# Scores and pair products of an SSD layer: when they are put into TensorE's stream of weight products, and in which order the weight blocks come

## The chip, the core and the metric

The kernel runs on one core of a Trainium2 chip. The metric is the device time of one execution in microseconds (us). Five engines work side by side, each through its own queue in program order: TensorE (PE, matrix products; its weight loads are listed as PEld), VectorE (DVE), ScalarE (ACT), GpSimd (POOL, here it mostly issues DMAs) and SyncE (SP, which issues the weight loads). An instruction waits at the head of its queue for the others' results, and everything behind it waits with it.

## The reference, cut to what matters

256 positions, width 2048: one Mamba-2 (SSD) layer of 64 heads in 8 groups, then keys and values and one attention layer, then a norm.

```python
def mamba2_layer(h, w_in, conv_w, conv_b, dt_bias, A_log, D_skip, gnorm_g, w_out):
    proj = h @ w_in                                  # 2048 x 10304
    z, xbc, dt = ...                                 # 4096, 6144 (x 4096, B 1024, C 1024), 64
    xbc = silu(causal_depthwise_conv(xbc, conv_w, conv_b))
    xs, bm, cm = ...                                 # 8 groups: x of 8 heads x 64, B and C of 128
    dt = softplus(dt + dt_bias); a = dt * -exp(A_log)
    y = ssd_chunked_scan(xs * dt, a, bm, cm)         # one chunk of 256
    y = y + D_skip * xs
    y = grouped_rmsnorm(y * silu(z), gnorm_g, 8)
    return y @ w_out                                 # 4096 x 2048

# in the scan, of the one chunk:
    a_cum = cumsum(ac, axis=1)
    decay = exp(where(causal, a_cum[l] - a_cum[s], -inf))      # per head
    cb = einsum("blgn,bsgn->blsg", cc, bc)                     # per group: the "scores"
    y_diag = einsum("blsgr,bsgrp->blgrp", cb * decay, xc)      # per head: the "pairs" multiply this

# reference(): x + mamba2_layer(rmsnorm(x)), then K and V of it, the attention layer, the last norm
```

## The kernel before, in words

**Weight products.** All weights are read from HBM once. A unit of work is one load of two 128-row slices of 512 columns (`load`, on SP, 512 KB). ACT rounds it to a reduced format (`hi`), DVE takes the rest (`lo`), both in `split`; then PE makes 12 products of 128x512 (`products`: two slices, two halves of the positions, and hi, lo and hi again against the two parts of the operand). In the trace these products are `ps<-hi,hT`, `ps<-lo,hT`, and with `yn`, `kvop`, `bop` or `oop` in place of `hT` for the later layers. Four raw buffers, five of `hi` and `lo`; splits are written three units ahead.

**Blocks.** `ORDER` (line 36) lists the blocks of the SSD layer. B, C, x, z and a number are 512 columns of the input projection, 8 units or 96 products each; d0 is the one of dt. o0 to o3 and o10 to o13 are quarters of the first half of the output projection, 4 units or 48 products each: o0 to o3 need the normed groups 0 and 1 (yn0, yn1), o10 to o13 need yn2 and yn3. p0 to p3 are the second half, 96 products each, which need yn4 to yn7. `late` (line 283) changes the start of p: first 6 units of p0, 6 of p1, then the last two units of each; so the first product that reads yn7 is product 144 after the start of p0.

**Side work.** Everything else of the layer is written as generators that `Side` advances between the products: `conv_gen` (convolution and SiLU of B, C and x, then x transposed and times dt, `xd`), `cb_gen` (the four score matrices of four groups, `cb`; PE reads C and B out of buffers named xs, so a visit to it reads `s<-xs`), `pair_gen` (two heads at a time: a DMA on POOL spreads the running sums over a buffer `em`, ACT makes the decays of it, DVE multiplies by the scores, PE makes the heads' output `s<-em,xd`, DVE adds D·x and multiplies by the gate z), `z_gen` (the gate), `norm_gen` (squares, a transposed sum `s<-ident,squares`, a chain of small DVE operations on `nt`, its result transposed back `s<-ident,nt`, the normed y into `yn`). There are two `em` buffers and four PSUM banks `s`. I call it a visit when PE leaves the products for such a piece and comes back.

**What sets the order.** While the program is written, a model keeps a time for PE, ACT and DVE (`Clock`, `Paced`), and `Side.some` (line 156) takes the next piece of a generator only where its last work ended, by the model, at least `MARGIN` (750 ns) before PE's time. A generator gives that time by what it last did itself, or by a number that it yields; where it yields a condition, the model knows only that it is fulfilled, not when the other generator's result is there. Before the products of a unit whose operand has not been written yet, all side work is forced through (line 1154): it is then put ahead of the unit, ready or not.

```python
            if entry[2] <= PE.ns - MARGIN:
                most -= self.advance(entry)
...
        if need not in st:
            force(lambda: need in st)
```

Of the kernel before, what the change touches and what calls it, by code (L numbers as in the profile page):

```python
# [15 lines left out]
P = 128  # L16
L = 256
# [15 lines left out]
MARGIN = 750.0  # L33


ORDER = "B0 d0 C0 x0 z0 x1 z1 x2 z2 x3 z3 B1 C1 x4 o0 z4 o1 x5 o2 z5 o3 x6 o10 z6 o11 x7 o12 z7 o13 p0 p1 p2 p3".split()
LOAD = 4700.0
WRITE = 5000.0
READ = 7000.0
# [132 lines left out]
def trunk_kernel(ctx: ExitStack, tc: tile.TileContext, x, a_norm_g, a_w_in, a_conv_w, a_conv_b,  # L172
# [3 lines left out]
    clock = Clock()  # L176
# [22 lines left out]
    PE = Paced(clock, nc.tensor, pe_cost, 0.0)  # L199
# [18 lines left out]
    B = {}  # L218
# [5 lines left out]
    def of(tag):  # L224
        return next(s for s in (banks, S[0], spare) if tag in s.shape)

    def can(*tags):
        return lambda: all(of(t).free(t) > 0 for t in tags)

    def take(tag):  # L230
        return of(tag).take(tag)
# [3 lines left out]
    def give(*tiles):  # L235

        for t in tiles:
            key = t.tensor.name, t.offset
            freed.append((next(s for s in (banks, S[0], spare) if key in s.held), key, clock.last))
# [17 lines left out]
    def copied(t, begin=0.0, issue=700.0):  # L257

        copies[0] = max(PE.ns, copies[0], begin) + issue
        clock.put(clock.writes, clock.part(t), copies[0] + READ, POOL)  # L260
        return copies[0] + READ
# [136 lines left out]
    def by_channel(U):  # L398

        return U.rearrange("p (b j l) -> p j b l", b=8, j=4)  # L400

    def in_32s(a):
        return a.rearrange("p j (b l) -> p j b l", l=32)
# [12 lines left out]
    em = take("em")  # L416
# [66 lines left out]
    for h in range(4):  # L483
        ACT.activation(early[:, 0, :512], xl[0][:, h * 512:(h + 1) * 512], AF.Square, accum_out=ss[:, 0, h:h + 1])
        v = xl[1][:, h * 512:(h + 1) * 512]
# [43 lines left out]
    hT = big.tile([P, 16, 2 * L], F32R, name="hT", tag="op")  # L529
    yn = {}  # L530
    st = {}

    def normed(i):

        c = slice(i * 512, (i + 1) * 512)
        DVE.tensor_scalar(xl[0][:, c], xl[0][:, c], r0[:, 0:1], None, op0=OP.mult)
        if i == 0:
            DVE.tensor_scalar(xl[1][:, c], xl[1][:, c], r0[:, 1:2], None, op0=OP.mult)
        else:
            ACT.activation(xl[1][:, c], xl[1][:, c], AF.Copy, scale=r0[:, 1:2])  # L540
# [63 lines left out]
    def conv_gen(U, there, c, key, group=None):  # L604

        yield there
        yield can("u", "xs")
        u, v = take("u"), take("xs")
        ACT.activation(in_32s(u), by_channel(U), AF.Copy)
        give(U)  # L610
        yield
        for j in range(4):
            k = 3 * 48 + c + j
            ACT.activation(v[:, j, :], u[:, j, :], AF.Identity, bias=cbias[:, c + j:c + j + 1], scale=cw[:, k:k + 1])
        for i in (1, 2, 3):
            yield
            for j in range(4):
                k = (3 - i) * 48 + c + j
                DVE.scalar_tensor_tensor(v[:, j, i:], u[:, j, :L - i], cw[:, k:k + 1], v[:, j, i:],
                                         op0=OP.mult, op1=OP.add)  # L620
        yield
        ACT.activation(u, v, AF.Tanh)
        yield
        DVE.scalar_tensor_tensor(v, u, 1.0, v, op0=OP.add, op1=OP.mult)
        give(u)
        st[key] = v
        if group is None:
            return
        yield lambda: "dal" in st and can("xd")()
        xd = take("xd")  # L630
        for i in (0, 2):
            yield can("s")
            p = take("s").rearrange("p (t c) -> p t c", t=2)
            for e in range(2):
                for t in range(2):
                    PE.transpose(p[:, t, e * P:(e + 1) * P], v[:, i + e, t * P:(t + 1) * P], ident)
            yield
            h = 2 * (c + i)
            DVE.tensor_mul(xd[:, :, i * P:(i + 2) * P].rearrange("p t (h c) -> p t h c", h=4),
                           p.rearrange("p t (h c) -> p t h c", h=4),  # L640
                           st["dal"][:, :, h:h + 4, None].to_broadcast([P, 2, 4, 64]))
            give(p)
        st["xd", group] = xd

    def conv_evac(c, key, group=None):
        def evac(ps, t):
            U, there = turn(ps, t)
            if t:
                side.add(conv_gen(U, there, c, key, group))
        return evac  # L650

    def cb_gen(q):
        B, C = st.pop(("B", q)), st.pop(("C", q))
        for j in range(4):
            yield can("s", "cb")
            p, cb = take("s")[:, :384], take("cb")
            PE.matmul(p[:, 0:256], lhsT=B[:, j, 0:P], rhs=C[:, j, :], start=True, stop=True)
            PE.matmul(p[:, 256:384], lhsT=B[:, j, P:L], rhs=C[:, j, P:L], start=True, stop=True)
            yield
            DVE.tensor_mul(cb, p, tri)  # L660
            give(p)
            st["cb", 4 * q + j] = cb
        give(B, C)

    def c_evac(q):
        base = conv_evac(40 + 4 * q, ("C", q))

        def evac(ps, t):
            base(ps, t)
            if t:  # L670
                side.add(cb_gen(q), lambda: ("B", q) in st and ("C", q) in st)
        return evac

    def pair_gen(g, j):

        c = 4 * g + j
        E = take("em")
        AC = st["AC"]
        R = bass.AP(tensor=AC.tensor, offset=AC.offset + 2 * c * L, ap=[[0, P], [L, 2], [1, L]])
        POOL.dma_start(E[:, :, :L], R)  # L680
        yield copied(E)
        yield lambda: "dal" in st
        dal = st["dal"]
        for h in range(2):
            a = 64 + 2 * c + h
            ACT.activation(E[:, h, 256:384], E[:, h, P:L], AF.Relu, bias=dal[:, 1, a:a + 1], scale=-1.0)
            ACT.activation(E[:, h, 0:256], E[:, h, 0:256], AF.Relu, bias=dal[:, 0, a:a + 1], scale=-1.0)
        ACT.activation(E, E, AF.Exp, scale=-1.0)
        yield lambda: ("cb", g) in st
        DVE.tensor_mul(E, E, st["cb", g][:, None, :].to_broadcast([P, 2, 384]))  # L690
        yield lambda: ("xd", g) in st and can("s")() and (("y", g) in st or can("yt")())
        xd, xs = st["xd", g], st["xs", g]
        q = take("s")[:, :L]
        for h in range(2):
            PE.matmul(q[h * 64:(h + 1) * 64, :], lhsT=xd[:, 0, j * P + h * 64:j * P + (h + 1) * 64],
                      rhs=E[:, h, 0:256], start=True, stop=False)
        for h in range(2):
            PE.matmul(q[h * 64:(h + 1) * 64, P:L], lhsT=xd[:, 1, j * P + h * 64:j * P + (h + 1) * 64],
                      rhs=E[:, h, 256:384], start=False, stop=True)
        give(E)  # L700
        if ("y", g) not in st:
            st["y", g], st["n", g] = take("yt"), 0
        yield
        y = st["y", g][:, j, :]
        DVE.scalar_tensor_tensor(y, xs[:, j, :], Dv[:, c:c + 1], q, op0=OP.mult, op1=OP.add)
        give(q)
        st["x", g] = st.get(("x", g), 0) + 1
        if st["x", g] == 4:
            give(xs, xd, st["cb", g])
        yield lambda: ("z", g) in st  # L710
        z = st["z", g]
        y = y.rearrange("p (b l) -> p b l", l=32)
        DVE.scalar_tensor_tensor(y, y, 0.5, by_channel(z)[:, j], op0=OP.mult, op1=OP.mult)
        st["n", g] += 1
        if st["n", g] == 4 and g not in (1, 3):
            give(z)
# [59 lines left out]
    def x_evac(g):  # L776
        base = conv_evac(4 * g, ("xs", g), g)

        def evac(ps, t):
            base(ps, t)  # L780
            if not t:
                return
            for j in range(4):
                side.add(pair_gen(g, j), lambda: "AC" in st and can("em")())
            side.add(norm_gen(g), lambda: st.get(("n", g)) == 4)
        return evac
# [23 lines left out]
    def x1_load():  # L810
        B["x1"] = [big.tile([P, D], F32, name=f"x1{t}", tag=f"y{7 - t}") for t in range(2)]
        for t in range(2):
            POOL.dma_start(B["x1"][t], xv[:, t])
        copies[0] = max(PE.ns, copies[0]) + 1200.0
        yield copies[0] + READ
        st["x1"] = True
# [73 lines left out]
    side.add(x1_load(), lambda: st.get(("n", 3)) == 4)  # L890
    for name in ORDER:
        kind, i = name[0], int(name[1:])
# [6 lines left out]
        else:  # L899
            n = i % 10  # L900
# [164 lines left out]
    for kind, n in ("z0", "q0", "z1", "q1", "z2", "q2", "q3", "z3"):  # L1065
        n = int(n)
# [136 lines left out]
```

## Time and profile before

| what | value |
|---|---|
| median of 3 runs | 1174.68 us (1172.6 to 1178.49) |
| the profiled execution's own time | 1174.74 us |
| its span, first to last instruction | 1173.0 us |
| PE busy | 1147.5 us, 98% of the span |
| PEld, DVE, ACT, POOL busy | 930.5, 835.0, 628.3, 107.2 us |
| PE in the chain that ended last | 87% |

The profile counts an engine as busy from an instruction's start to its modelled end, and PE's products overlap, so PE's 98% doesn't say that only 2% could be saved. What does is the distance between the starts of neighbouring products: where it is longer than in an undisturbed stretch, PE did something else or nothing. A bracket at the end of a row of the timeline is the time for which the engine stood idle before it and what ended that.

### The profile page before, as it was taken

The numbers are of one execution on the slowest core, as the hardware profiler recorded it, in microseconds if no ns is written. First come the engines' busy times: TensorE is split into PE (matmuls) and PEld (weight loads), VectorE is DVE, ScalarE is ACT, GpSimd is POOL, SyncE is SP. The second block draws the span as 40 slices with busy tenths as digits, with TensorE's granted clock in tenths as the row PEclk, the third lists the DMA queues.
The fourth block names the chain that finished last, engine by engine and source line by source line (L and its number), as shares of the span: only waits on it lengthen the run. The fifth ranks groups of instructions, "written<-read, shape, count | busy, mean of one in ns | idle before, by whom it ended". The sixth has DMA issues, their size and how long they took to land.

```text
span 1173.0 us, 14915 instructions
## 1 busy us (share of the span) xinstructions
PE 1147.5 (98%) x5285; PEld 930.5 (79%) x5285; DVE 835.0 (71%) x1275; ACT 628.3 (54%) x866; POOL 107.2 (9%) x185
## 2 busy tenths in 40 slices
PE   7999999999999999999998999999999999999996
PEld 4787877777778787887876888888888888888885
DVE  5786968788888678687776468777444677678564
ACT  5556565677656555655653555443443453544553
POOL 2011021111210011100010000000000000100000
PEclk9999999999999999999998999999999999999998
DMA  6787878778796777776774366778757767677552
GB/s 214 222 233 219 251 220 242 239 233 246 234 300 201 211 237 228 234 224 204 223 247 146 114 217 206 233 217 241 223 169 239 225 200 223 206 213 239 171 182 90
DMA packets 127658, 252.61 MB, mean 215 GB/s; under 512 B 12320, under 2 KB 12400, under 8 KB 127200
## 3 DMA queue, kind: packets, MB, share of 16 engines
q1 hardware_dynamic: 118064, 222.86, 60.5%
q0 software_dynamic: 9520, 28.81, 9.7%
q8 instruction: 41, 0.67, 0.2%
q14 instruction: 33, 0.27, 0.1%
HBM read 232.69 MB, written 18.94 MB: 215 GB/s over the span
## 4 chain that ended last, share of the span: by engine, by line
PE 87%; DMA 4%; DVE 4%; ACT 3%; issue 2%; SPq 0%; POOL 0%; ACTq 0%; DVEq 0%
PE ps L128 81%; PE s L128 6%; DMA raw<-in_a_w_in_dram 2%; DVE xs L128 1%; ACT hi L128 1%; DVE lo L128 1%; DMA raw<-in_a_w_out_dram 1%; ACT xs L128 1%; DMA U<-turned 1%; DMA turned<-T 0%; SPq L412 0%; DVE nt L128 0%; ACT em L128 0%; DVE T L128 0%; DVE yt L128 0%
## 5 line engine op out<-in xcount | busy, mean ns | idle before, releaser
L128 DVE TENSOR_TENSOR lo<-raw,hi 128x1024 fp32r<-128x1024 f32 x384 | 462.2, 1217 | 218.6 <-ACT hi L128 217.6
L128 ACT ACTIVATE hi<-raw 128x1024 fp32r<-128x1024 f32 x384 | 398.2, 1054 | 298.8 <-PE ps L128 181.2
L128 PE MATMUL ps<-hi,hT 128*128 128x512 f32 x1280 | 412.5, 395 | 0.1
L128 PEld LDWEIGHTS ps<-hi,hT 128*128 128x128 f32 x1280 | 240.3, 188 | 52.9 <-issue 3.6
L128 PE MATMUL ps<-lo,hT 128*128 128x512 f32 x640 | 249.6, 390 | 0.0
L128 PE MATMUL ps<-hi,yn 128*128 128x512 f32 x512 | 167.5, 398 | 3.0 <-ACT yn L128 2.9
L128 PE MATMUL ps<-hi,bop 128*128 128x512 f32 x512 | 164.0, 395 | 0.0
L128 PE MATMUL ps<-hi,kvop 128*128 128x512 f32 x512 | 159.0, 390 | 0.0
L394 POOL DMA_DIRECT2D U<-turned x128 | 74.2, 586 | 908.4 <-DMA turned<-T 482.4
L128 PEld LDWEIGHTS ps<-lo,hT 128*128 128x128 f32 x640 | 120.3, 188 | 23.0
L128 PEld LDWEIGHTS ps<-hi,yn 128*128 128x128 f32 x512 | 97.1, 190 | 24.6 <-ACT yn L128 3.2
L128 PEld LDWEIGHTS ps<-hi,kvop 128*128 128x128 f32 x512 | 96.1, 188 | 19.9
L128 PEld LDWEIGHTS ps<-hi,bop 128*128 128x128 f32 x512 | 96.1, 188 | 19.7
L128 PE MATMUL ps<-lo,yn 128*128 128x512 f32 x256 | 100.8, 394 | 0.0
L128 PE MATMUL ps<-lo,bop 128*128 128x512 f32 x256 | 99.7, 389 | 0.0
L128 PE MATMUL ps<-lo,kvop 128*128 128x512 f32 x256 | 99.6, 389 | 0.0
L128 PE MATMUL ps<-hi,oop 128*128 128x512 f32 x256 | 82.4, 395 | 0.0
L128 DVE SCALAR_TENSOR_TENSOR xs<-u,cw,xs 128x255 f32<-128x255 f32 (+2 forms) x144 | 59.9, 475 | 0.1
L128 PEld LDWEIGHTS ps<-lo,yn 128*128 128x128 f32 x256 | 48.7, 190 | 9.3
L128 ACT ACTIVATE em<-em,dal 128x128 f32<-128x128 f32 (+1 forms) x128 | 54.4, 448 | 2.9 <-DMA em<-AC 0.8
L128 PEld LDWEIGHTS ps<-hi,oop 128*128 128x128 f32 x256 | 48.1, 188 | 9.8
L128 PEld LDWEIGHTS ps<-lo,bop 128*128 128x128 f32 x256 | 48.1, 188 | 9.6
(168 smaller groups left out, 903.4 us busy)
## 6 DMA issues: line engine op xcount, KB each, us to landing
raw<-in_a_w_in_dram SPq DMA_DIRECT2D x160, 512.0 KB, 5.4
raw<-in_a_w_out_dram SPq DMA_DIRECT2D x64, 512.0 KB, 4.8
raw<-in_w_kv_dram SPq DMA_DIRECT2D x64, 512.0 KB, 4.7
raw<-in_b_w_in_dram SPq DMA_DIRECT2D x64, 512.0 KB, 4.6
turned<-T SPq DMA_DIRECT2D x64, 256.0 KB, 4.7
U<-turned POOLq DMA_DIRECT2D x128, 128.0 KB, 5.5
raw<-in_b_w_out_dram SPq DMA_DIRECT2D x32, 512.0 KB, 4.5
em<-AC POOLq DMA_DIRECT2D x32, 256.0 KB, 6.7
```

Of the source, the lines that this page charges most:

```text
L128: return call(out, *args, **kw)
L394: POOL.dma_start(U[32 * q:32 * q + 32].rearrange("p (b c) -> p b c", b=8), src)
```

## The change

Three edits. `ORDER`: from x4 on, each z block comes before the o block that it stood behind, so that o0 to o12 move one place back; o12 and o13 now both follow z7. `cb_gen`: a wait in the model until both operands are ready by its clock (`when`), in place of the bare condition that they have been written. `pair_gen`: of two neighbouring pairs, the even one stops after the multiplication by the scores; the odd one waits, in the model, for `xd` and the even one's result, then for two free banks, and makes the products of both; each goes on by itself from its own bank.

```diff
-ORDER = "... z3 B1 C1 x4 o0 z4 o1 x5 o2 z5 o3 x6 o10 z6 o11 x7 o12 z7 o13 p0 p1 p2 p3".split()
+ORDER = "... z3 B1 C1 x4 z4 o0 x5 o1 z5 o2 x6 o3 z6 o10 x7 o11 z7 o12 o13 p0 p1 p2 p3".split()
...
-        st[key] = v
+        st[key], when[key] = v, clock.last
...
-        st["xd", group] = xd
+        st["xd", group], when["xd", group] = xd, clock.last
...
         B, C = st.pop(("B", q)), st.pop(("C", q))
+        yield max(when["B", q], when["C", q])
...
         DVE.tensor_mul(E, E, st["cb", g][:, None, :].to_broadcast([P, 2, 384]))
-        yield lambda: ("xd", g) in st and can("s")() and (("y", g) in st or can("yt")())
-        xd, xs = st["xd", g], st["xs", g]
-        q = take("s")[:, :L]
...
+        st["em", g, j], when["em", g, j] = E, clock.last
+        if j % 2:
+            yield lambda: ("xd", g) in st and ("em", g, j - 1) in st
+            yield max(when["xd", g], when["em", g, j - 1])
+            yield lambda: of("s").free("s") > 1 and (("y", g) in st or can("yt")())
+            for i in (j - 1, j):
+                xd, E, q = st["xd", g], st.pop(("em", g, i)), take("s")[:, :L]
...
+                give(E)
+                st["q", g, i], when["q", g, i] = q, clock.last
...
+        else:
+            yield lambda: ("q", g, j) in st
+            yield when["q", g, j]
+        xd, xs, q = st["xd", g], st["xs", g], st.pop(("q", g, j))
```

**On PE, the first scores.** Second half of block z0. Before, the first score product (`s_953<-xs_802,xs_557`: C and B of the first four groups) stands right behind the last product of the unit `hi_871`:

```order
L128 MATMUL ps_860<-lo_872,hT_130 128x512
L128 MATMUL ps_860<-hi_871,hT_130 128x512
L128 MATMUL s_953<-xs_802,xs_557 128x256
L128 MATMUL s_953<-xs_802,xs_557 128x128
L128 MATMUL ps_849<-hi_893,hT_130 128x512
```

After, six products of the next unit (`hi_893`) stand ahead of it:

```order
L128 MATMUL ps_860<-lo_872,hT_130 128x512
L128 MATMUL ps_860<-hi_871,hT_130 128x512
L128 MATMUL ps_849<-hi_893,hT_130 128x512
L128 MATMUL ps_849<-lo_894,hT_130 128x512
L128 MATMUL ps_849<-hi_893,hT_130 128x512 x2
L128 MATMUL ps_849<-lo_894,hT_130 128x512
L128 MATMUL ps_849<-hi_893,hT_130 128x512
L128 MATMUL s_965<-xs_802,xs_557 128x256
L128 MATMUL s_965<-xs_802,xs_557 128x128
```

The score visit moved back by six products. The other stretch with scores (groups 4 to 7) starts 12 products into z4 before, 78 products into z4 after; counted in products from the layer's start that is 18 later.

**On PE, a group's pairs.** Block x2. Before, one pair to a visit; behind these rows 16 more products come before the next pair (`s_1521<-em_1310,xd_1195`):

```order
L128 MATMUL ps_1445<-hi_1385,hT_130 128x512
L128 MATMUL s_1480<-em_1303,xd_1195 64x256 x2
L128 MATMUL s_1480<-em_1303,xd_1195 64x128 x2
L128 MATMUL ps_1438<-hi_1403,hT_130 128x512
L128 MATMUL ps_1438<-lo_1404,hT_130 128x512
```

After, the same two pairs in one visit:

```order
L128 MATMUL ps_1437<-hi_1431,hT_130 128x512
L128 MATMUL s_1519<-em_1321,xd_1240 64x256 x2
L128 MATMUL s_1519<-em_1321,xd_1240 64x128 x2
L128 MATMUL s_1524<-em_1328,xd_1240 64x256 x2
L128 MATMUL s_1524<-em_1328,xd_1240 64x128 x2
L128 MATMUL ps_1454<-hi_1431,hT_130 128x512
```

The 32 pairs take 27 visits before (22 of one pair, 5 of two) and 16 visits of two pairs after.

**On ACT, the last group's norm.** Blocks p0 and p1. ACT writes one `hi` for each unit of 12 products. Before, from the `hi` of the unit that starts 144 products after the start of p0 (`hi_5392`, the first unit that reads yn7) on:

```order
L128 ACTIVATE hi_5392<-raw_5298 128x1024
L128 ACTIVATE squares_5412<-yt_5203 128x1024
L128 ACTIVATE hi_5414<-raw_5326 128x1024
L128 ACTIVATE hi_5434<-raw_5346 128x1024
L128 ACTIVATE hi_5455<-raw_5366 128x1024
L128 ACTIVATE yn7_5483<-yt_5203 128x4x256
L128 ACTIVATE hi_5511<-raw_5396 128x1024
```

After, from the `hi` of the unit that starts 108 products after the start of p0 (`hi_5324`); `hi_5401` is the one of the unit at 144:

```order
L128 ACTIVATE hi_5324<-raw_5244 128x1024
L128 ACTIVATE squares_5358<-yt_5170 128x1024
L128 ACTIVATE hi_5360<-raw_5267 128x1024
L128 ACTIVATE hi_5380<-raw_5291 128x1024
L128 ACTIVATE hi_5401<-raw_5310 128x1024
L128 ACTIVATE hi_5434<-raw_5328 128x1024
L128 ACTIVATE hi_5460<-raw_5364 128x1024
L128 ACTIVATE yn7_5459<-yt_5170 128x4x256
L128 ACTIVATE hi_5480<-raw_5384 128x1024
```

The squares moved ahead by three units and `yn7` by one. On PE, counted in products ahead of the first product that reads yn7: the visit with the last pairs moved from 39 to 69, that of the transposed squares from 3 to 39, that of the transposed `nt` from 0 to 18.

## Rows read from the trace of the kernel before

**Rows 1.** Page, parts 1 and 5: busy time and share; the costliest DVE group.

```profile
PE 1147.5 (98%) x5285; PEld 930.5 (79%) x5285; DVE 835.0 (71%) x1275; ACT 628.3 (54%) x866; POOL 107.2 (9%) x185
...
L128 DVE TENSOR_TENSOR lo<-raw,hi 128x1024 fp32r<-128x1024 f32 x384 | 462.2, 1217 | 218.6 <-ACT hi L128 217.6
```

**Rows 2.** Waits of PE: who waited for whom, us in total, times, longest.

```profile
PE ps L128 <- ACT yn L128: 2.9, 1, 2.9
PE s L128 <- DVE xs L128: 2.7, 2, 1.4
```

**Rows 3.** Timeline of PE, undisturbed products (start, length, engine, line, what, shape, count).

```profile
302.23 0.40 PE L128 MATMUL ps<-lo,hT 128*128 128x512 f32 x1
...
311.76 0.39 PE L128 MATMUL ps<-lo,hT 128*128 128x512 f32 x1
```

**Rows 4.** Timeline of PE, p0 and p1, around the first product with yn7.

```profile
622.69 1.52 PE L128 MATMUL s<-em,xd 128*64 128x256 f32 x16
...
632.21 0.39 PE L128 MATMUL ps<-hi,yn 128*128 128x512 f32 x1
632.44 0.38 PE L128 MATMUL s<-ident,squares 128*128 128x128 f32 x2
...
632.89 0.40 PE L128 MATMUL ps<-lo,yn 128*128 128x512 f32 x1
633.12 0.40 PE L128 MATMUL ps<-hi,yn 128*128 128x512 f32 x1
636.02 0.40 PE L128 MATMUL s<-ident,nt 128*128 128x128 f32 x2 [2.50 <-DVE nt L128]
639.34 0.79 PE L128 MATMUL ps<-hi,yn 128*128 128x512 f32 x1 [2.92 <-ACT yn L128]
...
645.15 0.40 PE L128 MATMUL ps<-lo,yn 128*128 128x512 f32 x1
```

**Rows 5.** Busy time by engine in a stretch; then granted clock, DMA share, GB/s.

```profile
640.00:650.00 10.00, 9.96 (x35) 7.59 (x34) 4.49 (x6) 2.97 (x5) 0.00 (x0) 0.76 0.16 52
```

**Rows 6.** Timeline of PE, three score visits: one that waited, one more, one undisturbed.

```profile
105.69 0.39 PE L128 MATMUL ps<-hi,hT 128*128 128x512 f32 x1
107.52 0.92 PE L128 MATMUL s<-xs 128*128 128x256 f32 x4 [1.44 <-DVE xs L128]
108.20 0.48 PE L128 MATMUL ps<-hi,hT 128*128 128x512 f32 x1
...
351.37 0.92 PE L128 MATMUL s<-xs 128*128 128x256 f32 x4 [1.22 <-DVE xs L128]
...
353.97 0.39 PE L128 MATMUL ps<-hi,hT 128*128 128x512 f32 x1
...
354.76 0.47 PE L128 MATMUL ps<-hi,hT 128*128 128x512 f32 x1
```

**Rows 7.** Timeline of PE, pair visits: of one, of one that waited, of two.

```profile
169.85 0.39 PE L128 MATMUL ps<-hi,hT 128*128 128x512 f32 x1
...
171.31 0.40 PE L128 MATMUL ps<-lo,hT 128*128 128x512 f32 x1
...
221.59 0.87 PE L128 MATMUL s<-em,xd 128*64 128x256 f32 x8 [0.21 <-issue]
...
413.65 0.39 PE L128 MATMUL ps<-hi,yn 128*128 128x512 f32 x1
...
415.76 0.40 PE L128 MATMUL ps<-lo,yn 128*128 128x512 f32 x1
```

**Rows 8.** Timelines of POOL, ACT and DVE: one refill of an `em` buffer.

```profile
604.01 0.71 POOL L680 DMA_DIRECT2D em<-AC  x1 [2.33 <-ACT hi L128]
613.45 1.76 ACT L128 ACTIVATE em<-em,dal 128x128 f32<-128x128 f32 x4
615.24 0.85 ACT L128 ACTIVATE em<-em 128x768 f32<-128x768 f32 x1
619.35 1.82 DVE L128 TENSOR_TENSOR em<-em,cb 128x768 f32<-128x768 f32 x2
```

More of the change, by code (lines that the diff above doesn't have):

```diff
@@ L33 @@
 MARGIN = 750.0
-ORDER = "B0 d0 C0 x0 z0 x1 z1 x2 z2 x3 z3 B1 C1 x4 o0 z4 o1 x5 o2 z5 o3 x6 o10 z6 o11 x7 o12 z7 o13 p0 p1 p2 p3".split()
+ORDER = "B0 d0 C0 x0 z0 x1 z1 x2 z2 x3 z3 B1 C1 x4 z4 o0 x5 o1 z5 o2 x6 o3 z6 o10 x7 o11 z7 o12 o13 p0 p1 p2 p3".split()
 LOAD = 4700.0
@@ L531, in trunk_kernel @@
     st = {}
+    when = {}
     def normed(i):
@@ L690, in pair_gen @@
         DVE.tensor_mul(E, E, st["cb", g][:, None, :].to_broadcast([P, 2, 384]))
-        yield lambda: ("xd", g) in st and can("s")() and (("y", g) in st or can("yt")())
-        xd, xs = st["xd", g], st["xs", g]
-        q = take("s")[:, :L]
[L694 to L703, printed above, removed]
+        st["em", g, j], when["em", g, j] = E, clock.last
[5 more added lines that the diff above has]
+                xd, E, q = st["xd", g], st.pop(("em", g, i)), take("s")[:, :L]
+                for h in range(2):
+                    PE.matmul(q[h * 64:(h + 1) * 64, :], lhsT=xd[:, 0, i * P + h * 64:i * P + (h + 1) * 64],
+                              rhs=E[:, h, 0:256], start=True, stop=False)
+                for h in range(2):
+                    PE.matmul(q[h * 64:(h + 1) * 64, P:L], lhsT=xd[:, 1, i * P + h * 64:i * P + (h + 1) * 64],
+                              rhs=E[:, h, 256:384], start=False, stop=True)
+                give(E)
+                st["q", g, i], when["q", g, i] = q, clock.last
+            if ("y", g) not in st:
+                st["y", g], st["n", g] = take("yt"), 0
+            yield
+        else:
+            yield lambda: ("q", g, j) in st
+            yield when["q", g, j]
+        xd, xs, q = st["xd", g], st["xs", g], st.pop(("q", g, j))
         y = st["y", g][:, j, :]
```

## The prediction

> **What bounds the kernel now.** I read the page's busy times first: PE is busy for 98% of the span, and every other engine for less than 80% [rows 1]. So the time is what PE's queue takes, and only two things shorten it: less work on PE, or fewer stretches in which PE stands still. Then the list of what PE waited for: it is short, and three kinds of wait matter here, one for `yn`, one for `nt` (it stands in the timeline) and two for xs, the operands of the scores [rows 2, 4]. Busy time can't price them, since PE's rows overlap. So I went to PE's timeline and took the distance between starts. In an undisturbed stretch 42 products start within 9.53 us, 0.2269 us each [rows 3]. Whatever lies between two product starts beyond that is the price of a visit or a wait, and that price is measured three times below: at the last norm, at the scores, at the pairs.
>
> **The change part by part.** The products, transposes, splits, loads and DMAs are the same in number and shape; only places on the queues change. So each term is a stretch of PE's timeline that gets shorter.
>
> *The last norm.* From the product at 633.12 to the one at 645.15 there are 12.03 us, in which 14 products start (13 of them from 639.34 on); at 0.2269 they take 3.18 [rows 4]. The visit of a transposed `nt` in between costs about what the one of the squares does, 0.68 us less two products, 0.23 [rows 4]. The rest, 8.62 us, is lost. It has two parts: from 639.34 to 645.15 the 13 products take 5.81 us in place of 2.95, so 2.86 us go to a slower clock (the mean granted clock from 640 to 650 is 0.76 [rows 5], so part of that stretch ran at the lower level, 1.2 GHz, after PE had stood still twice, for 2.50 and for 2.92 us); 5.76 us are the two waits themselves.
>
> They are one chain: last pairs at 622.69, squares turned at 632.44, `nt` turned at 636.02, the first product with yn7 at 639.34 [rows 4]: 16.65 us from first to last, 3.58 and 3.32 us for the last two links. In the old order only 39 products lie ahead of the needing product when the chain begins, and nothing at all at its end. In the new one it is 69 at the last pairs, 39 at the squares and 18 at `nt`. In time: 69 × 0.2269 = 15.66, plus the pair visit (1.66, below) and two transposing visits of 0.23, 17.8 us, against the 16.65 that the chain took; squares to `nt` 21 products and a visit, 5.0 us, against 3.58; `nt` to the need 18 and a visit, 4.3, against 3.32. Each link has about 1 us to spare. What is late next is the low part of yn7, a DVE operation that the third product of the unit needs; DVE has one more `lo` split (1.22 us [rows 1]) ahead of it than before, while ACT writes the high part. I leave 0.2 us of wait for it, and the clock stays up. Gain 8.4 us; bounds 0 (the chain is as late as it was) and 8.6. Why it comes earlier at all: x7 and z7 end 48 products earlier, by the new order of blocks, while the start of p0 stays where it is.
>
> *The scores.* The undisturbed score visit takes 0.79 us between the starts around it, the one that waited 2.51: 1.72 lost [rows 6]. The second one that waited stood idle for 1.22 in place of 1.44, so it lost about 1.50 [rows 6]. The first visit now stands six products later, 1.36 us, which leaves 0.36 of its wait; DVE's and ACT's queues are the same up to there. The second stands 18 products later, 4.1 us, more than it waited. Gain 1.36 + 1.50 = 2.9 us; bounds 0 and 3.2. Who waits for the later scores? Only DVE's multiplication of the decays, and in the old order the first pair stood 156 products behind the first scores. That covers it.
>
> *Pairs two to a visit.* From the product ahead of a visit to the second behind it: 1.46 us with one pair, 2.11 with two [rows 7]; less two products, 1.01 and 1.66. Two pairs in one visit save 2.01 − 1.66 = 0.36 us. 22 single visits become 11 double ones: 3.9 us. One single visit had waited for 0.21 us besides [rows 7]; that goes too, if the margin of the new waits holds. Gain 4.1; bounds below. The Trainium skill, "TensorE: Matmul & The Clock Gate", section "The cost: per-tile semaphore tail", gives the end of a group of small products as 25 ns, plus 4.7 for each tile and 26.3 for each semaphore increment; as an estimate from that, with two tiles and one increment, a visit saved would bring 61 ns, 11 of them 0.7 us, and the sum would come out 3.2 us higher. The five visits of two pairs that the trace has speak against it, at 0.36 us.
>
> The new waits could cost as well. An odd pair that waits in the model holds no engine, for it isn't in a queue yet. But once it stands on PE and one of its two `em` isn't ready, all products behind it wait. And both buffers now come back at one visit, so both DMAs, two times four ACT passes with an exponential and two multiplications must fit between two visits of pairs. A refill took, from the issue at 604.01 to the end of the exponential at 616.09, 12.1 us, and a multiplication 0.91 (half of 1.82) [rows 8]; the second buffer adds one ACT pass of 2.61 (1.76 and 0.85): 15.6 us. The shortest distance of two pair visits in the new order is 90 products, 20.4 us. It fits with 4.8 to spare, so I take 0; the bounds are 0 and the rival's price below. The other moved blocks (each z a place earlier, each o a place later) give the normed groups 0 to 3 more time before o needs them, and PE waited for none of those before; x, z, x, z without an o between them is how groups 0 to 3 ran. I cost them at nothing.
>
> **Sum.** 8.4 + 2.9 + 4.1 = 15.4 us. The profiled execution took 1174.74 us, as long as the median of the three runs (1174.68), so 1174.7 − 15.4 = **1159.3 us**. If nothing of the waits is left, 8.6 + 3.2 + 4.1 = 15.9 give 1158.8; the lowest run of before lies 2.1 below the median, which makes 1156.5 the low end.
>
> **Rivals.**
>
> 1. *The last norm is late all the same.* For it: the links have 1 us to spare, about one `lo` split, and where DVE is behind, each further split puts 1.22 us into the chain. A wait of 1 to 2 us gives 1160.5 to 1161.5; two waits as long as now would bring the low clock back, and with all 8.4 us the time is 1167.7. Against it: the chain keeps its order on DVE and ACT, and its first link alone has 69 products in place of 39.
>
> 2. *The paired visits wait, and it gets slower.* Place: the 16 visits, each with everything behind it on PE. Cause: the multiplication of the second `em` sits in DVE's queue behind splits, as at 619.35, 3.3 us after its exponential had ended [rows 8]. It decides from 15.4 / 16 = 0.96 us a visit on. With one split (1.22 us) each it costs 19.5 us, and the time is 1179; half of that would give 1169, no change to speak of. Against it: 3.3 us late at 619.35 still let the visit at 622.69 begin without a wait, and the model's margin kept all but one of the single visits from waiting.
>
> 3. *The model's waits don't help the scores*, because the chip's DVE is later than the model's: the two waits move along and stay, 1162.2. For it: the first one keeps 0.36 us even by my working. Against it: 18 products at the second are far more than its 1.5 us.
>
> **How the numbers follow.** My forecast, within 1156.5 to 1161.5: 0.62. The last norm late, 1161.5 to 1168: 0.17. The scores as before, around 1162: 0.06. Some waiting at the pairs: 0.10, half of it below 1168.8, half at no change. Waiting at all pairs, slower: 0.05. A measurement of this kernel tells 0.5%, 5.9 us, from no change: faster means below 1168.8. Faster then has 0.62 + 0.17 + 0.06 + 0.05 = 0.90, no change 0.05, slower 0.05. The range reaches from 1156.5 to 1167, which leaves out the last bit of rival 1, half of the waiting pairs and rival 2.
>
> **What would show it.** In the profile after: around the first product with yn7 the starts stay 0.23 us apart, no bracket of 2 us, and the granted clock stays at 1.00 from 600 to 660. The score visits take 0.79 us between the products around them (the first up to 1.2). All pair visits read x16 and cost 1.66 us; a bracket on them is rival 2. p2 and everything behind it starts about 15 us earlier and is otherwise as before: attention isn't touched. I am wrong if PE's products wait at a place where they didn't before, or if the gap at yn7 is still above 2 us.

## The result, and the profile after

The changed kernel takes 1158.31 us in the median of four runs (1158.11 to 1158.39), the kernel before on the same chip 1175.06 us (1172.6 to 1178.49). The ratio is 0.9855, with a 95% interval of 0.983 to 0.988, so it is 1.2 to 1.7% faster: inside the range, and 1.0 us below the forecast of 1159.3. The profiled execution took 1158.11 us, its span 1156.3, which is 16.7 us less than the span before.

The page after: busy time and share of each engine, and the chain that ended last by engine. The first line answers to [rows 1].

```profile
PE 1140.4 (99%) x5285; PEld 930.7 (80%) x5285; DVE 835.6 (72%) x1275; ACT 628.9 (54%) x866; POOL 106.7 (9%) x185
...
PE 98%; DMA 1%; SPq 0%; DVE 0%; ACT 0%; issue 0%; ACTq 0%
```

The counts in the first line are those of before, and of its busy times only PE's has changed by more than 0.6 us (7.1 less). PE's share of the chain has gone from 87% to 98%. What PE waited for (us in total, times, longest), in answer to [rows 2]; all of it lies ahead of the first product, and the rows for `yn`, `nt` and xs are gone:

```profile
PE s L128 <- DMA xl<-in_x_dram: 3.3, 2, 2.5
PE s L128 <- DMA ga<-in_a_norm_g_dram: 2.7, 1, 2.7
PE s L128 <- DVE xl L128: 0.3, 1, 0.3
```

Timeline after, in answer to [rows 6], [rows 7] and [rows 4]: the first score visit, a pair visit, and from the last pairs to the products with yn7 (PE; then the ACT operation that writes yn7's high part; then, on DVE, the sums of the squares, the last operation on `nt` and yn7's low part):

```profile
106.79 0.39 PE L128 MATMUL ps<-hi,hT 128*128 128x512 f32 x1
107.02 0.81 PE L128 MATMUL s<-xs 128*128 128x256 f32 x4
107.58 0.47 PE L128 MATMUL ps<-hi,hT 128*128 128x512 f32 x1
...
171.97 0.39 PE L128 MATMUL ps<-hi,hT 128*128 128x512 f32 x1
172.29 1.52 PE L128 MATMUL s<-em,xd 128*64 128x256 f32 x16
173.74 0.50 PE L128 MATMUL ps<-hi,hT 128*128 128x512 f32 x1
174.07 0.40 PE L128 MATMUL ps<-lo,hT 128*128 128x512 f32 x1
...
607.76 1.52 PE L128 MATMUL s<-em,xd 128*64 128x256 f32 x16
...
616.14 0.38 PE L128 MATMUL s<-ident,squares 128*128 128x128 f32 x2
...
621.17 0.38 PE L128 MATMUL s<-ident,nt 128*128 128x128 f32 x2
...
625.26 0.62 PE L128 MATMUL ps<-hi,yn 128*128 128x512 f32 x2
625.71 0.39 PE L128 MATMUL ps<-lo,yn 128*128 128x512 f32 x1
625.94 0.62 PE L128 MATMUL ps<-hi,yn 128*128 128x512 f32 x2
...
623.34 1.06 ACT L128 ACTIVATE yn<-yt 128x1024 fp32r<-128x1024 f32 x1 [2.22 <-DVE yt L128]
...
613.69 1.15 DVE L128 TENSOR_TENSOR squares<-squares 128x512 f32<-128x512 f32 x2
...
619.65 0.16 DVE L128 SCALAR_TENSOR_TENSOR nt<-nt 128x2 f32<-128x2 f32 x1
...
624.44 1.23 DVE L128 TENSOR_TENSOR yn<-yt,yn 128x1024 fp32r<-128x1024 f32 x1
```

The score visit takes 0.79 us between the starts of the products around it, as the undisturbed one did before, and doesn't wait. The pair visit takes 2.10 us from the product ahead to the second behind, as the double visits before did, and all 16 of them do. The products with yn7 begin at the second one of the row at 625.26, 0.23 us apart, with no bracket. Every link of the chain is in time: the squares were ready at 614.84, 1.3 us ahead of their visit, `nt` at 619.81, 1.4 us ahead, yn7's high part at 624.40, 1.1 us ahead, and the low part at 625.67, 0.3 us ahead of the third product at 625.94. The granted clock stayed up, in answer to [rows 5] (stretch, busy us and count of PE, PEld, DVE, ACT, POOL, then clock, DMA share, GB/s):

```profile
620.00:630.00 10.00, 10.00 (x46) 8.24 (x46) 7.57 (x10) 5.20 (x5) 0.00 (x0) 1.00 0.58 185
```

Where the 16.7 us came from, each visit priced as in the prediction (distance of the products around it, less 0.227 us; one profiled execution of each kernel):

| part | before | after | less | forecast |
|---|---|---|---|---|
| visit of `nt` ahead of yn7 | 5.99 | 0.14 | 5.85 | 5.76 |
| lower clock behind it | 2.86 | 0 | 2.86 | 2.86 (with 0.2 of new wait: 8.4 in all) |
| the two score visits that waited | 2.28 + 2.06 | 0.57 + 0.57 | 3.2 | 2.9 |
| all pair visits, with 0.11 at the product behind each | 30.7 | 26.4 | 4.2 | 4.1 |
| first product of the kernel | 17.21 | 16.94 | 0.3 | – |

That is 16.4 of 16.7 us; 0.3 are not assigned.

### The profile page after: what moved, and what is told of

Its sections match the earlier page's. It is cut to its first block, busy times and chain, and to the rows that moved or that the text cites. A ratio compares the mean times of both kernels' runs of the same rounds, so it can differ in the third digit from the quotient of the medians.

```text
span 1156.3 us, 14912 instructions
## 1 busy us (share of the span) xinstructions
PE 1140.4 (99%) x5285; PEld 930.7 (80%) x5285; DVE 835.6 (72%) x1275; ACT 628.9 (54%) x866; POOL 106.7 (9%) x185
## 4 chain that ended last, share of the span: by engine, by line
PE 98%; DMA 1%; SPq 0%; DVE 0%; ACT 0%; issue 0%; ACTq 0%
PE ps L128 91%; PE s L128 6%; DMA raw<-in_a_w_in_dram 1%; PE ps_dt L128 0%; SPq L412 0%; DVE sfin L128 0%; ACT hi L128 0%; DVE xl L128 0%; DVE nt L128 0%; ACT T L128 0%; ACT x L128 0%; DVE x L128 0%; ACTq L1209 0%; ACT hT L128 0%; SPq L407 0%
## 5 line engine op out<-in xcount | busy, mean ns | idle before, releaser
L128 DVE STREAM_TRANSPOSE T<-ps 128x512 f32<-128x512 f32 x64 | 44.1, 706 | 20.2 <-PE ps L128 19.8
L128 PEld LDWEIGHTS ps<-lo,kvop 128*128 128x128 f32 x256 | 48.1, 188 | 9.7
```

The source lines that it names most:

```text
L128: return call(out, *args, **kw)
```

## The experiments

After the forecast had come true, what was left to doubt was its form: three terms, each put down to one part of the change and added up. **ADDING** says that each edit brings its term wherever it stands. **COVER** says that an edit alone also moves the last pairs of group 7, so that the wait for yn7 grows or shrinks with the products that lie between these pairs and the need. The times below are medians against the kernel before on the same chip (1173.5 to 1173.9 us there).

| run | what it is | us | ratio, 95% interval |
|---|---|---|---|
| e_blocks | order of blocks alone | 1165.4 | 0.9929, 0.9913–0.9945 |
| e_scores | waits of the scores alone | 1178.6 | 1.0044, 1.0029–1.0059 |
| e_pairs | pairs two to a visit alone | 1182.7 | 1.0081, 1.0057–1.0105 |
| e_noblocks | all but the order | 1182.4 | 1.0075, 1.0058–1.0092 |
| e_nopairs | all but the pairs | 1163.2 | 0.9911, 0.9897–0.9926 |
| e_noscores | all but the scores | 1160.8 | 0.9898, 0.9881–0.9915 |
| e_swap | e_noblocks, z4 moved | 1168.8 | 0.9966, 0.9953–0.9979 |
| e_late | e_noblocks, last blocks moved | 1167.2 | 0.9946, 0.9931–0.9961 |
| e_cover | after, 12 products less of cover | 1161.5 | 0.9898, 0.9884–0.9911 |
| e_fill | before, PE kept busy in the gap | 1171.7 | 0.9985, 0.9976–0.9994 |
| e_four | after, four pairs to a visit | 1161.5 | 0.9896, 0.9877–0.9914 |
| after_again | after | 1158.4 | 0.9872, 0.9858–0.9885 |

**Each edit alone, and the other two without the order.** e_blocks is the kernel before with the changed `ORDER` line, e_noblocks the changed kernel with the old one. e_scores and e_pairs are the kernel before with these hunks of the change:

```diff
# e_scores
+        yield max(when["B", q], when["C", q])
# e_pairs
+        if j % 2:
+            yield lambda: ("xd", g) in st and ("em", g, j - 1) in st
...
+            for i in (j - 1, j):
```

> The kernel before with the new order of blocks alone. Two theories for all four of these runs. COVER: what PE loses at the first product with yn7 is the chain from the last pair visit to yn7 (16.65 us in the trace of before) less what lies on PE between them (0.2269 us a product, 1.66 a visit of two pairs, 0.23 a transposing visit), where that is positive, and 2.9 us of lower clock once it is; the edits share that place. ADDING: the three edits bring 8.4, 2.9 and 4.1 us each by itself, whatever the others are. Here, in the built order, the last pairs stand 78 products ahead of the need, the score visits and the 27 pair visits where they were. COVER: no wait at yn7, 1174.7 - 8.6 = 1166.1 us, score visits still wait 1.7 and 1.5. ADDING: 1166.3, the same.

> The kernel before with the model's wait for the score operands alone. In the built order the last pairs stand 27 products ahead of the need (39 before), and as a side effect 11 visits hold two pairs and 10 hold one (5 and 22 before). COVER: idle at yn7 16.65 - 27 x 0.2269 - 1.66 = 8.9 us in place of 5.8, so + 3.1; scores - 2.9; six visits fewer - 2.1 and the late one - 0.2: 1172.6 us. ADDING: 1174.7 - 2.9 - 2.3 = 1169.5, idle at yn7 as before.

> The kernel before with the pairs two to a visit alone. In the built order the last pairs stand 12 products ahead of the need; the second score visit that waited stands 24 products later, the first where it was. COVER: idle at yn7 16.65 - 12 x 0.2269 - 1.66 = 12.3 us, + 6.5; pairs - 4.1; second score wait - 1.5: 1175.6 us, no faster than before. ADDING: 1174.7 - 4.1 - 1.5 = 1169.1.

> The changed kernel with the old order of blocks. In the built order the last pair visit stands right at the first product with yn7, so that the whole chain is uncovered. COVER: idle there 16.65 - 1.66 = 15.0 us, + 9.2 against before; pairs and scores - 7.0: 1176.9 us, slower than before although two of the three edits are in. ADDING: 1174.7 - 7.0 = 1167.7.

The order alone came out as expected, at 8.2 us less, and the gap at yn7 was gone. The other two edits made the kernel slower without it, alone and together, which ADDING excludes. But they also came out 5 to 7 us above COVER. The trace of e_noblocks shows two places that lose time (PE at yn7; then POOL's issue of a load, behind four other issues; then DVE's additions that need the load, and behind them the operation that writes the operands of the scores):

```profile
634.27 1.52 PE L128 MATMUL s<-em,xd 128*64 128x256 f32 x16
639.80 0.66 PE L128 MATMUL s<-ident,squares 128*128 128x128 f32 x2 [4.01 <-DVE squares L128]
643.45 0.66 PE L128 MATMUL s<-ident,nt 128*128 128x128 f32 x2 [2.98 <-DVE nt L128]
647.02 0.80 PE L128 MATMUL ps<-hi,yn 128*128 128x512 f32 x1 [2.92 <-ACT yn L128]
...
336.82 2.31 POOL L394 DMA_DIRECT2D U<-turned  x4 [21.38 <-ACT hi L128]
339.13 1.13 POOL L824 DMA_DIRECT2D x<-in_x_dram  x2
...
348.83 0.69 DVE L128 TENSOR_TENSOR x<-ps,x 128x512 f32<-128x512 f32 x1 [5.39 <-DMA x<-in_x_dram]
352.15 0.69 DVE L128 TENSOR_TENSOR x<-ps,x 128x512 f32<-128x512 f32 x1 [2.63 <-DMA x<-in_x_dram]
...
355.70 1.22 DVE L128 SCALAR_TENSOR_TENSOR xs<-u,xs 128x1024 f32<-128x1024 f32 x1
```

The load and the additions in the kernel before:

```profile
320.99 0.57 POOL L813 DMA_DIRECT2D x<-in_x_dram  x1
327.49 0.56 POOL L813 DMA_DIRECT2D x<-in_x_dram  x1 [5.94 <-DVE yt L128]
...
347.69 1.29 DVE L128 TENSOR_TENSOR x<-ps,x 128x512 f32<-128x512 f32 x2
```

At yn7 no product is left between the last pairs and the need, and the whole chain lies open: the visit costs 12.8 us, 11.0 more than its work, and the lower clock follows.

The second place is one that the prediction had not looked at. The residual x is loaded in two pieces of 1 MB into buffers that `x1_load` asks for once the last pairs of group 3 have been multiplied by the gate; o0's results are added to it. With paired visits this multiplication ends later (at 333.65, before at 327.20). Besides, the load now stands in POOL's queue behind four other issues, at which POOL stood until 336.82. So it is issued 12 to 18 us later than before, and 5.5 us of that (333.65 to 339.13) are the place in POOL's queue. In the old order o0 doesn't move: DVE stands still for 5.39 and 2.63 us, behind it in DVE's queue is what the scores of groups 4 to 7 need, and the score visit at 350 costs 8.01 us in place of 0.57. As an estimate from these times, with the load ahead of the four issues and as long on its way, DVE would have waited about 5 us less; no run here shows it.

The 24.3 us by which this span exceeds the one of after are 11.0 at yn7, 7.4 at that visit, and 5.8 at products that follow each other too slowly (the lower clock behind both gaps, and a wait of 1.0 for the low part of yn6).

In e_pairs the same two places are late: DVE waits for the load for 5.26 and 2.61 us, and the score visit costs 7.86. In e_scores yn7 is late too, but the score visits are not; PE stands still ahead of the transposed squares of group 3:

```profile
348.55 0.66 PE L128 MATMUL s<-ident,squares 128*128 128x128 f32 x2 [5.54 <-ACT u L128]
```

This visit stands 42 products into o0, between the two halves of its last unit. There, in `out_evac`, the kernel forces all side work through until the load of x has been asked for, ready or not. The last pairs of group 3 come 18 us later than before (339.87, before 321.53), so their squares are late; DVE's sums of them end at 348.40. DVE's waits for the load, 1.38 and 2.53 us, come only behind that. It is the same need of o0 for x, reached in another way; that the forcing put the visit there is read from the program and the visit's place, not tested.

And the gap at yn7 follows the cover. With 69 products between the last pairs and the need (after) PE stands idle for 0 us there, with 39 (before) for 5.8, with 27 (e_scores) for 7.6, with 21 (e_swap, below) for 7.8, with 12 (e_pairs) for 9.9, with none for 11.0. COVER's direction holds, its sizes do not: it expected 8.9, 12.3 and 15.0 us in e_scores, e_pairs and e_noblocks. It took the chain's 16.65 us as fixed, and the chain gets shorter when less other work stands in DVE's and ACT's queues: in e_noblocks it takes 12.8.

**Which of the two places, one at a time.** Two orders between the old and the new, with the other two edits in. TWO PLACES says that each place costs by itself, ONE PLACE that yn7 explains it all.

```diff
# e_swap: z4 ahead of o0
-x4 o0 z4 o1 x5 o2 z5 o3 x6 o10 z6 o11 x7 o12 z7 o13
+x4 z4 o0 o1 x5 o2 z5 o3 x6 o10 z6 o11 x7 o12 z7 o13
# e_late: the last blocks
-x4 o0 z4 o1 x5 o2 z5 o3 x6 o10 z6 o11 x7 o12 z7 o13
+x4 o0 z4 o1 x5 o2 z5 o3 x6 o10 z6 x7 o11 z7 o12 o13
```

> The kernel of e_noblocks (pairs and score waits in, old order of blocks) with one exchange in the order: z4 before o0; everything from o1 on stands where it stood. TWO PLACES: the old order has two deadlines that the other two edits miss, the load of x (issued when group 3's last pairs are through, 339 to 346 us, first needed when o0 is added to it) and yn7. Then this exchange alone takes away the wait near 350 us: 8.01 - 0.57 us at the score visit and about 1.9 us of lower clock, 9.3 us in all; the last pairs stand 21 products ahead of the need for yn7, so by the runs with 0, 12, 27 and 39 products (11.0, 9.9, 7.6 and 5.8 us idle) 8.5 us stay there: 1182.4 - 9.3 - 2.5 and up to 1.5 for yn6 = 1169 to 1171 us. ONE PLACE (only yn7 matters, and the wait near 350 comes of the pairs or score visits themselves): the wait near 350 stays, 1179.

> The kernel of e_noblocks with the other half of the change of order: x4 o0 z4 ... as before up to z6, then x7 o11 z7 o12 o13, so that x7 and z7 come earlier and o0 doesn't come later. In the built order the last pairs stand 81 products ahead of the need for yn7. TWO PLACES: no wait at yn7 and none at yn6, 11.0 + 1.5 us of waits and 2.7 of lower clock less, but the wait for x near 350 us stays with its 9.3: 1182.4 - 15.2 = 1167.2 us. ONE PLACE: 1158.3, as the changed kernel.

Both fell within 0.2 us of where TWO PLACES put them: 13.6 us are saved by z4 ahead of o0, 15.2 by the last blocks, each from e_noblocks. e_swap has no wait near 350 and still one at yn7; e_late is the other way round. The two savings add up to 28.8 us, more than the 24.1 that the whole order brings, because they overlap: z4 ahead of o0 also leaves 21 products between the last pairs and yn7 where e_noblocks has none, and takes 3.2 us of its saving there and about 1 at yn6. In e_late PE's score visit, and DVE ahead of it:

```profile
358.14 1.65 PE L128 MATMUL s<-xs 128*128 128x256 f32 x4 [6.94 <-DVE xs L128]
...
350.01 0.69 DVE L128 TENSOR_TENSOR x<-ps,x 128x512 f32<-128x512 f32 x1 [5.81 <-DMA x<-in_x_dram]
353.32 0.69 DVE L128 TENSOR_TENSOR x<-ps,x 128x512 f32<-128x512 f32 x1 [2.62 <-DMA x<-in_x_dram]
```

PE's bracket names DVE, and DVE's names the load: the load is two steps back.

**Scores and pairs, taken out of the new order.** e_noscores is the changed kernel without the `yield max(...)` of `cb_gen`, e_nopairs the one with the old end of `pair_gen`:

```diff
# e_nopairs
-        if j % 2:
...
-            for i in (j - 1, j):
+        yield lambda: ("xd", g) in st and can("s")() and (("y", g) in st or can("yt")())
```

> The changed kernel with one pair to a visit: order of blocks and score waits in. In the built order 22 visits of one pair and 5 of two, as in the kernel before, and the last pairs 75 products ahead of the need for yn7. If a visit costs 0.36 us by itself and the order of blocks covers both deadlines: 1158.3 + 11 x 0.36 = 1162.2 us, no wait on PE. If the pairs bring nothing of their own (0.06 us a visit): 1159.

> The changed kernel without the model's wait for the score operands. In the built order the first score visit is back behind the unit that it stood behind before, six products earlier; the second stands 12 products later than in the kernel before. If only the score operands were late: the first waits again, 0.4 (as in e_pairs) to 1.7 us, the second up to 1.5: 1158.7 to 1161.5 us. No wait at yn7.

e_nopairs is 4.8 us above the changed kernel. 3.9 and one late visit (0.24) make 4.2 of it, as its pair visits in the trace do; the other 0.6 aren't assigned. e_noscores is 2.4 to 2.5 above it, and its trace shows three score visits that lose 0.40, 0.56 and 1.56 us. So in the new order each edit does bring its term. A single pair visit in e_nopairs (start, length):

```profile
168.18 0.39 PE L128 MATMUL ps<-hi,hT 128*128 128x512 f32 x1
168.50 0.87 PE L128 MATMUL s<-em,xd 128*64 128x256 f32 x8
169.30 0.50 PE L128 MATMUL ps<-hi,hT 128*128 128x512 f32 x1
169.64 0.40 PE L128 MATMUL ps<-lo,hT 128*128 128x512 f32 x1
```

**What a visit costs, with four pairs.** Two more `em` buffers, in a place that is free until x is loaded, for groups 0 to 3:

```diff
+    more = Parts(big, "emx", "y7", [P, 2, 384], 2)
...
-        E = take("em")
+        E = take("emx" if g < 4 and j > 1 else "em")
...
+        n = 4 if g < 4 else 2
-        if j % 2:
+        if j % n == n - 1:
```

> The changed kernel with four pairs to a visit in groups 0 to 3 (two more em buffers, in a place of SBUF that is free until x is loaded); groups 4 to 7 as they were. 12 visits in place of 16; in the built order the last pairs and the norm behind them stand within three products of where they stood. If a visit costs 0.36 us by itself, whatever it holds: 1.4 us less than the changed kernel, 1156.9 us. If the gain of two to a visit came of something that four don't repeat, or the four buffers that come back at once are late: 1158.3 or more, with a wait on PE at a pair visit.

> The changed kernel once more, on the same chip as the three others, to compare them with: 1158.3 us.

e_four came out 3 us above after_again in place of below it (1158.6 to 1163.5 in five runs). In the profiled one the visits did what was expected; another place lost more (PE: a visit of four pairs, then the score visit; POOL's load of x; ACT):

```profile
148.87 0.39 PE L128 MATMUL ps<-hi,hT 128*128 128x512 f32 x1
149.19 1.52 PE L128 MATMUL s<-em,xd 128*64 128x256 f32 x16
150.54 1.47 PE L128 MATMUL s<-emx,xd 128*64 128x256 f32 x16
151.94 0.50 PE L128 MATMUL ps<-hi,hT 128*128 128x512 f32 x1
...
348.12 1.65 PE L128 MATMUL s<-xs 128*128 128x256 f32 x4 [2.57 <-DVE xs L128]
...
315.71 1.13 POOL L827 DMA_DIRECT2D x<-in_x_dram  x2
...
327.67 1.06 ACT L128 ACTIVATE hi<-raw 128x1024 fp32r<-128x1024 f32 x1 [7.08 <-DMA raw<-in_a_w_in_dram]
```

From product to product the visit of four takes 3.07 us, 2.84 of its own, against 2 × 1.54 for two visits; with the 0.11 at the product behind, 0.35 us are saved for each visit that goes, as at one against two. But x is now loaded at 315.71 (339.84 in after), ACT then stands still for 7.08 us until a load of weights has landed, and 20 us later the scores wait for DVE; that visit costs 4.04 us in place of 0.57. That the one delay leads to the other is argued from their order; no run here moved the load alone.

**Less cover at the last norm.** In the changed kernel `late` puts three units in place of two at the end, so the first product with yn7 comes 12 products earlier.

```diff
-        late(blocks[n_out], 8, 2)
+        late(blocks[n_out], 8, 3)
```

> The changed kernel with 12 products less between the start of p0 and the first product with yn7 (five units of p0 and five of p1 ahead instead of six and six); all else stands where it stood up to there. In the profile of the changed kernel the transposed nt starts at 621.17 and yn7's high part is ready at 624.40, its low part at 625.67. COVER: six products behind the transposed nt the need comes at 622.8; PE waits 1.6 us for the high part and up to 0.8 for the low part: 1159.9 to 1160.7 us, and with waits that short the lower clock doesn't come back. If yn7 had several us to spare after the change: 1158.3, no wait.

It lost 3.1 us against after_again. The two waits are about those that were expected, and behind them the products stand 0.43 us apart from 626.3 to 629.7, at a granted clock of 0.50, which was not (PE, then the stretch as above):

```profile
624.51 0.50 PE L128 MATMUL ps<-hi,yn 128*128 128x512 f32 x1 [1.52 <-ACT yn L128]
624.85 0.40 PE L128 MATMUL ps<-lo,yn 128*128 128x512 f32 x1
625.77 0.77 PE L128 MATMUL ps<-hi,yn 128*128 128x512 f32 x2 [0.53 <-DVE yn L128]
626.34 0.63 PE L128 MATMUL ps<-lo,yn 128*128 128x512 f32 x1
626.77 1.05 PE L128 MATMUL ps<-hi,yn 128*128 128x512 f32 x2
...
620.00:630.00 10.00, 7.95 (x29) 5.72 (x28) 6.16 (x8) 3.07 (x3) 0.00 (x0) 0.83 0.55 186
```

**The clock's share, by itself.** In the kernel before, PE gets eight products that nothing reads, four ahead of the transposed `nt` and four behind it (each is two rows in the trace), so that it doesn't stand still while yn7 comes:

```diff
+        if fill:
+            dummy(4)     # nc.tensor.matmul(t[:, :384], lhsT=ident, rhs=tri)
```

> The kernel before with eight products that nothing reads (128x384 in float32, 0.64 us each) put where PE stands still at yn7: four ahead of the transposed nt, where it idled 2.50 us, four behind it, where it idled 2.92. They take nothing away from the wait. If the slower products after the wait come of PE having stood still: the gap of 6.2 us stays (up to 0.3 longer), the products behind it start 0.23 us apart at once, and 2.9 us go: 0.9975 of before, 1171 us. If they are slower for another reason (the operand yn7 just written, DMA): no change.

The ratio is 0.9985; the 0.9975 that was expected lies just outside the interval. PE at yn7, and the stretch behind it:

```profile
634.22 2.75 PE L1146 MATMUL s<-tri,ident 128*128 128x384 f32 x8
637.29 0.50 PE L128 MATMUL ps<-hi,yn 128*128 128x512 f32 x1 [0.33 <-ACT yn L128]
...
638.55 0.74 PE L128 MATMUL ps<-hi,yn 128*128 128x512 f32 x2 [0.52 <-DVE yn L128]
...
640.00:650.00 10.00, 10.00 (x46) 8.21 (x46) 4.74 (x6) 4.16 (x6) 0.00 (x0) 1.00 0.43 144
```

yn7 comes no earlier: from the product ahead of the gap to the first one with yn7 it is 6.22 us in both traces. But the clock stays at 1.00 where it was 0.76 [rows 5]. The 2.86 us go, and 0.7 us of wait for yn7's low part come, which the slow products had hidden before: about 2.2 are left, and that is what was missed.

## Why the prediction was right, and where it was not

**The method.** The distance between product starts held: priced by it, the stretches that the prediction named hold 16.1 of the 16.7 us. Rivals 1 and 2 are out, by the traces: no wait at yn7, none at any of the 16 pair visits (every second multiplication ended at least 1.7 us ahead of its visit). Rival 3 is out too, since the score visits didn't wait. Two small sums of the prediction are off by 0.2 us: 1158.8 less 2.1 is 1156.7, and waits of 1 to 2 us on top of 1159.3 give 1160.3 to 1161.3; nothing hangs on either.

**The last norm: right in time and mechanism.** The term was 8.4, the trace gives 8.7. The 0.2 us for the low part of yn7 were not needed, by 0.3 us. The split in 5.76 of wait and 2.86 of clock [rows 4, 5] is what e_fill shows from the other side. "About 1 us to spare" was right at each link: 1.3, 1.4 and 1.1 us in the trace after, and from the last pairs to yn7's high part it took 16.6 us (607.76 to 624.40), as long as before. With 12 products less, 2.7 us, e_cover waited for 1.5.

**The scores: right, but one of the two waits was sized from a single execution.** The second wait [rows 6] was there in each run with the old condition. The first one, 1.72 us in the trace before, was 0.2 in e_blocks and 0.1 in e_fill, where PE's order is the same up to there, and 0.4 in e_pairs and e_noscores. So it is partly luck that the table has 3.2 us here; in the new order the edit is worth 2.4 us, by e_noscores.

**The pairs: right.** 0.36 us for each visit saved was read from single and double visits [rows 7]; visits of four go on with 0.35. The 61 ns a visit that were estimated from the Trainium skill, "TensorE: Matmul & The Clock Gate", section "The cost: per-tile semaphore tail", would make e_nopairs 0.7 us slower than the changed kernel; it is 4.8 slower.

**The step that was wrong** is "I cost them at nothing", of the other moved blocks. The prediction asked only whether the normed groups come in time for o, not the load of x, whose start hangs on group 3's last pairs and whose end o0 needs. It did no harm to the number, because the order edit moved that deadline back as well (o0's additions are at 369.76 in after, 347.69 before) and the load, issued 19 and 13 us later, landed by 352.8. For the prediction that was luck: it had the number right without having looked. And the sum has a term for each edit, as if each could be had alone. Measured in the old order the scores bring +5.1 and the pairs +9.1 us; in the new one −2.4 and −4.8. The order alone brings −8.2, on top of the others −24.1. Pairing and waiting delay the results of a group; the order of blocks is what pays for that, at o0 and at yn7.

## What to carry to other kernels

A change that makes visits fewer by letting work wait for its neighbour also makes its results later: before summing the gains, list who needs these results last, the transfers that start when they are through among them, and count the work that still lies ahead of each. Test parts of a change alone and taken out of the whole; where the two disagree, they share a deadline. And follow a wait to its end: PE's row named DVE, DVE's named a load, and the load had started late because its group was late and because other issues stood ahead of it in its queue.

## What was not expected of the hardware

The granted clock fell after less standing still than I had thought: in e_cover two waits of 1.52 and 0.53 us, with two products between them, were followed by products 0.43 us apart from 626.3 to 629.7, 1.6 us more than at the full clock; the granted clock was 0.50 there, the lower level of 1.2 GHz. In the kernel before it fell behind waits of 2.50 and 2.92 us, in e_late behind one of 6.94; in e_blocks, behind a single wait of 1.7 us at a score visit, it stayed at 1.00. Useless products in the gap kept the clock at 1.00 and were worth about 2 us (2.2 in the trace and between the medians, 1.8 by the ratio).
